# Recurrent mixer of an encoder: score blocks of a forward and a backward direction issued in one run on TensorE, the first run of each pair keeping only its lowest level

## The chip, the cores and the metric

The kernel runs on one NeuronCore of a Trainium2 chip. The metric is the device time of one launch in microseconds (us). The time of the kernel before is the median of three runs, 2628.89 us (2628.30 to 2629.09). About 0.2% of that, 5.3 us, is what a measurement of this kernel can tell from no change.

## The reference, cut to what matters

The kernel computes a two-layer encoder on 1024 tokens of width 1024. Layer 0 is a windowed attention, layer 1 a bidirectional gated linear recurrence; each layer also has four cross-attention heads into 256 memory tokens, and ends with a convolutional gated feed-forward part. Only layer 1's recurrence and its cross-attention heads matter here. The recurrence runs for 8 heads of 128 key and 128 value dimensions, once forward and once backward in time:

```python
def gla_chunked(q, k, v, log_f):
    ...
    b = jnp.cumsum(log_f, axis=2)
    b_end = b[:, :, -1:]
    q_dec = q * jnp.exp(b)
    k_dec = k * jnp.exp(-b)
    k_end = k * jnp.exp(b_end - b)
    causal = np.tril(np.ones((HG_CHUNK, HG_CHUNK), dtype=bool))
    s = jnp.where(causal, jnp.einsum('bcthk,bcshk->bchts', q_dec, k_dec), 0.0)
    o_intra = jnp.einsum('bchts,bcshv->bcthv', s, v)

    def step(state, inp):
        qd, ke, vc, dec = inp
        o = jnp.einsum('bthk,bhkv->bthv', qd, state)
        state = dec[..., None] * state + jnp.einsum('bshk,bshv->bhkv', ke, vc)
        return state, o
...
    o = (gla_chunked(q, k_f, v, lf_f)
         + flip_t(gla_chunked(flip_t(q), flip_t(k_b), flip_t(v), flip_t(lf_b))))
    o = rmsnorm(o, norm_g.reshape(HG_HEADS, HG_VAL_DIM)).reshape(bsz, t, HG_W).astype(u.dtype)
    o = o * jax.nn.silu(gate)
```

All operands are float32.

## The kernel before, in words

The whole program is unrolled in Python and given to a scheduler, which fixes the order of each engine's queue when the program is built: among the instructions whose inputs and buffers are there it takes the one that stands earliest in the program, and `tc.high_priority(AHEAD)` moves instructions ahead by 2000 places. Buffers are named by pool and tag, with a number of copies (`bufs`); the next tile of a tag waits until a copy's last reader is done. Large matrix products are made in three passes of a high and a low part of each operand (`mm3`, lines 84 to 86), because both operands are split into two fp32r tiles.

Layer 1's mixer is `hgrn()` (from line 1023). It goes head by head. `proj(h)` (from line 1137) makes the head's projections in groups of 24 matmuls of 512 columns each: `q` and the two gates `s` (called f and b in `ORD`), each for two halves of 512 tokens, and, for every second head, the values and output gates of two heads. Every group writes a bank of PSUM with the tag `pj`, of which there are two (`psj`, line 1041). A bank is free again when the group's result was read: for `q` by three ScalarE operations and a VectorE multiplication (lines 1091 to 1093 and 1129), for `s` by one VectorE operation (line 1134).

`head(h)` (line 1338) then calls `direction` four times in this order of (direction, half): (0,0), (1,1), (0,1), (1,0); I call these runs 1 to 4. One run computes, for 512 tokens in four chunks `c` of 128, the decay factors on ScalarE and VectorE (lines 1177 to 1228), then the scores of each chunk. The 128x128 score matrix of a chunk is triangular and is built from three levels of blocks: four 32x32 blocks on the diagonal (from `E2` and `E1`; the lowest level), two 32x32 blocks beside them (from `G32`), and one 64x64 block (from `G`) written as two blocks of 32 rows and 64 columns. Each block is one fp32 matmul with 32 rows of output, at one of four column strips of TensorE (`tile_position=(0, i)`, line 1212):

```python
                return pe.matmul(pa[i:i + 32, c, j:j + n], x[:, c * P + i:c * P + i + 32], y[:, c * P + j:c * P + j + n],
                                 start=True, stop=True, tile_position=(0, i))
```

Strip number i/32 is the place of the block's output rows. Lines 1231 to 1246 issue eight blocks a chunk, 32 a run: first, chunk by chunk, the two 64-column blocks, the two diagonal blocks of the other half of the rows and one middle block there; then, again chunk by chunk, the other two diagonal blocks and the other middle block. In one run the 64-column blocks lie in two of the four strips, `far` and `near`: strips 3 and 2 for direction 0, strips 0 and 1 for direction 1. So the strip `far` gets, for each chunk, one block of 64 columns and two of 32, the strip beside it one of 64 and one of 32, and the other two strips two blocks and one block of 32.

After that a masked copy moves the scores from PSUM to `Az` (line 1253, VectorE), and they are stored or added to `As` of the half (line 1257 ScalarE, or 1259 GpSimd). The keys are transposed (line 1262), multiplied with the values (line 1267), and the state `S` is updated on VectorE (line 1276). `output` (line 1279), called for half 1 and then half 0 after all four runs, multiplies `As`, `qin` and `S` (line 1291) into a bank `po`, normalizes, and writes the result.

The decay factors use a ring of five tiles with the tag `E`; a run takes eight of them (`a_`, `L1`, `R`, `B`, `E1`, `E2`, and `G` twice).

Between the runs of every second head stand two units of the cross-attention (`cross`, line 1327; `cross_unit` from line 201): one after run 3, one after run 4. A unit makes its queries in a `pj` bank (24 matmuls), splits them into `xh` and `xl` (lines 214 and 215), multiplies with the memory keys (tile `ps`), takes the softmax, transposes it (line 237), splits it twice into `ph` and `pl` (lines 89 and 90, once for each half of the memory tokens), and multiplies with the memory values (tile `po` or `pu`). `xh`, `xl`, `ph` and `pl` have one buffer each.

The functions that the change touches, with what calls them:

Of the kernel before, what the change touches and what calls it, by code (L numbers as in the profile page):

```python
# [8 lines left out]
F32 = mybir.dt.float32  # L9
F32R = mybir.dt.float32r  # L10
# [3 lines left out]
ALU = mybir.AluOpType  # L14
# [4 lines left out]
P = 128  # L19
# [30 lines left out]
def build(tc, A, out):  # L50
    nc = tc.nc
    act, dve, pool, pe = nc.scalar, nc.vector, nc.gpsimd, nc.tensor
# [970 lines left out]
    def hgrn():  # L1023
# [3 lines left out]
        early = tc.alloc_tile_pool(name="hg0", bufs=1, reuse_waits="tile")  # L1027
# [4 lines left out]
        late = tc.alloc_tile_pool(name="hgv", bufs=1, side="right", reuse_waits="tile")  # L1032
        V, G = [late.tile([P, 3, NT, P], F32, name=x) for x in ("v", "gs")]
        wp = tc.alloc_tile_pool(name="hg1", bufs=1, side="right", reuse_waits="tile")
        for x in ("xh", "xl", "ph", "pl"):
            wp.tile([P, 512], F32R, tag=x, bufs=1, name=x)
        for x in ("kvh", "kvl"):
            wp.tile([P, 2, 256], F32R, tag=x, bufs=1, name=x)
# [22 lines left out]
        gm = [one([P, 512], f"gm{d}", U8) for d in range(2)]  # L1061
# [20 lines left out]
        Az = [one([P, 512], f"Az{d}") for d in range(2)]  # L1082
# [12 lines left out]
        def proj_tm(h, us, ts):  # L1095
# [3 lines left out]
            for t in ts[::2]:  # L1099
# [37 lines left out]
        def proj(h):  # L1137

            r = {"q": [None, None], "s": [[None, None], [None, None]], "v": V[:, h % 3], "gs": G[:, h % 3]}
            us = {}  # L1140
# [18 lines left out]
            r["run"] = run  # L1159
            return r  # L1160

        def direction(h, r, d, b, qin, S, As):

            q, k = r["q"][b], r["s"][d][b]
            rev = slice(None, None, -1) if d else slice(None)
            lt, er = (0, 1) if d else (1, 0)

            def E():
                return early.tile([P, 512], F32, tag="E", bufs=5, name="E")

# [22 lines left out]
            pa = PA[d]  # L1193
            E1, E2 = E(), E()
# [5 lines left out]
            def parts(n):  # L1200
                return halves(EP, n) + halves(ER, n) + halves(q, n) + halves(k, n)
# [8 lines left out]
            def block(c, i, j, x, y, n=32):  # L1210

                return pe.matmul(pa[i:i + 32, c, j:j + n], x[:, c * P + i:c * P + i + 32], y[:, c * P + j:c * P + j + n],
                                 start=True, stop=True, tile_position=(0, i))

            def step(n):
                pl_, pe_, rl_, re_ = parts(n)[:4]
                e = 0 if d else n - 1
                nb = 512 // (2 * n)
                dve.tensor_tensor(re_, re_, bc(pl_[:, :, e:e + 1], [P, nb, n]), op=ALU.mult)
                dve.tensor_tensor(pl_, pl_, bc(pe_[:, :, e:e + 1], [P, nb, n]), op=ALU.mult)  # L1220

            for n in (32, 64):
                step(n // 2)
                G = E()
                gl, ge = halves(G, n)
                pl_, pe_, rl_, re_, ql, qe, kl, ke = parts(n)
                pool.tensor_tensor(gl, pl_, ql, op=ALU.mult)
                dve.tensor_tensor(ge, re_, ke, op=ALU.mult)
                if n == 32:
                    G32 = G  # L1230
            with tc.high_priority(AHEAD):
                far, near, x = er * 64 + er * 32, er * 64 + lt * 32, lt * 64
                mm = None
                for c in range(4):
                    with tc.issue_after(mm.ins) if mm else nullcontext():
                        block(c, far, x, G, G, 64)
                        block(c, near, x, G, G, 64)
                        for o in (0, 32):
                            block(c, x + o, x + o, E2, E1)
                        mm = block(c, x + er * 32, x + lt * 32, G32, G32)  # L1240
                for c in range(4):
                    with tc.issue_after(mm.ins):
                        block(c, far, far, E2, E1)
                        block(c, near, near, E2, E1)
                        mm = block(c, far, near, G32, G32)
            step(64)
            dec = wp.tile([P, 4], F32, tag="dec", bufs=2, name="dec")
            e = 0 if d else P - 1
# [4 lines left out]
            dve.copy_predicated(Az[d], gm[d], pa.rearrange("p c t -> p (c t)"))  # L1253
            a2 = lambda x: x.rearrange("p c t -> p (c t)")
            if As[b] is None:
                As[b] = wp.tile([P, 4, P], F32, tag="As", bufs=2, name="As")
                act.copy(a2(As[b]), Az[d])
            else:
                pool.tensor_tensor(a2(As[b]), a2(As[b]), Az[d], op=ALU.add)
            tp = bank("pt")  # L1260
            for c in range(4):
                pe.transpose(tp[:, c, :], ER[:, c * P:(c + 1) * P], ident)
# [5 lines left out]
            for c in (range(3, -1, -1) if d else range(4)):  # L1268
                cg = 4 * b + c
                nx = cg - 1 if d else cg + 1  # L1270
                if not 0 <= nx < NT:
                    continue
                if cg == (NT - 1 if d else 0):
                    act.copy(S[:, nx, :], pu[:, c, :])
                else:
                    dve.scalar_tensor_tensor(S[:, nx, :], S[:, cg, :], dec[:, c:c + 1], pu[:, c, :],
                                             op0=ALU.mult, op1=ALU.add)

        def output(h, r, b, qin, S, As):
            po = bank("po")  # L1280
# [45 lines left out]

        def cross(n):
            def pair(kind, i):
                return [wp.tile([P, 512], F32R, tag=kind + c, bufs=1, name=kind + c) for c in "hl"]

            for _ in range(n):
                xh_, xb_ = units.pop(0)
                if xhead[1] != xh_:
                    xhead[1] = xh_
                    xhead[0] = cross_head(1, xh_, wp)
                cross_unit(1, xh_, xb_, xhead[0], wp, tags, wp, pair, not units)

# [239 lines left out]
```

## Time and profile before

| What | Value |
|---|---|
| median of 3 runs | 2628.89 us |
| the profiled execution: its own time | 2632.24 us |
| its span, first to last instruction | 2630.4 us |
| granted TensorE clock, mean | 0.998 |
| PE busy over the span | 2593.7 us (99%) |
| DVE busy | 1763.4 us (67%) |
| ACT busy | 1333.4 us (51%) |
| POOL busy | 476.4 us (18%) |
| layer 1's recurrent mixer in the span | from about 1208 to 1890 us |

PE is TensorE's matmul side, PEld its loading of weights, DVE is VectorE, ACT ScalarE, POOL GpSimd. In a row of the time line the first number is the start in us from the span's beginning, the second the duration; then come engine, line, operation, the tiles written and read, and their shapes. A fp32 matmul appears as two records, a weight load and a matmul twice over, so that a run's 32 blocks are 64 matmul records. A row of a query by line gives the count, the shortest, median and longest duration in ns, and the first and last start. The ends of matmuls are modelled, so their starts say more than their durations.

### The profile page before, as it was taken

The numbers are of one execution on the slowest core, as the hardware profiler recorded it, in microseconds if no ns is written. First come the engines' busy times: TensorE is split into PE (matmuls) and PEld (weight loads), VectorE is DVE, ScalarE is ACT, GpSimd is POOL, SyncE is SP. The second block draws the span as 40 slices with busy tenths as digits, with TensorE's granted clock in tenths as the row PEclk, the third lists the DMA queues.
The fourth block names the chain that finished last, engine by engine and source line by source line (L and its number), as shares of the span: only waits on it lengthen the run. The fifth ranks groups of instructions, "written<-read, shape, count | busy, mean of one in ns | idle before, by whom it ended". The sixth has DMA issues, their size and how long they took to land. (4 is left out here: it accounts for less than half of the span.)

```text
span 2630.4 us, 39132 instructions
## 1 busy us (share of the span) xinstructions
PE 2593.7 (99%) x14596; PEld 2174.2 (83%) x14596; DVE 1763.4 (67%) x2807; ACT 1333.4 (51%) x2395; POOL 476.4 (18%) x552
## 2 busy tenths in 40 slices
PE   8999999999999999999999999999999999999998
PEld 7988887888888888887888888888887888888887
DVE  6677775577555664488697796877657665656447
ACT  6566665444444454465555554556434444444453
POOL 0431110211111100032233131222311011110013
PEclk9999999999999999999999999999999999999999
DMA  9782341567787757673246341113337777775666
GB/s 356 258 199 67 103 146 57 168 171 195 192 210 201 198 160 250 194 267 109 70 151 162 75 99 47 55 49 101 120 119 197 190 201 200 205 200 172 215 193 236
DMA packets 203919, 431.18 MB, mean 164 GB/s; under 512 B 20048, under 2 KB 64464, under 8 KB 198096
## 3 DMA queue, kind: packets, MB, share of 16 engines
q1 hardware_dynamic: 169744, 329.30, 38.4%
q0 software_dynamic: 24544, 90.19, 16.4%
q10 hardware_dynamic: 9440, 9.19, 1.1%
q8 instruction: 114, 1.87, 0.3%
q14 instruction: 77, 0.63, 0.1%
HBM read 333.18 MB, written 119.54 MB: 172 GB/s over the span
## 5 line engine op out<-in xcount | busy, mean ns | idle before, releaser
L90 DVE TENSOR_TENSOR wl<-st,wh 128x1024 fp32r<-128x1024 f32 (+1 forms) x238 | 263.3, 1113 | 318.8 <-ACT wh L89 294.4
L89 ACT CAST wh<-st 128x1024 fp32r<-128x1024 f32 (+1 forms) x238 | 222.6, 937 | 293.1 <-PE X L578 194.1
L84 PE MATMUL pj<-uh,wh 128*128 128x512 f32 x512 | 202.9, 397 | 3.6 <-DVE q L1129 2.5
L578 PE MATMUL X<-wl,wh 128*128 128x512 f32 x528 | 204.7, 390 | 0.3 <-DVE wl L90 0.3
L578 PE MATMUL X<-wh,wl 128*128 128x512 f32 x528 | 204.5, 389 | 0.0
L86 PE MATMUL pj<-uh,wl 128*128 128x512 f32 x512 | 202.1, 395 | 0.0
L85 PE MATMUL pj<-ul,wh 128*128 128x512 f32 x512 | 201.0, 393 | 0.1
L578 PE MATMUL X<-wh 128*128 128x512 f32 x528 | 198.7, 390 | 1.4 <-ACT c L992 1.4
L84 PE MATMUL pj<-wh,uh 128*128 128x384 f32 (+1 forms) x512 | 189.0, 370 | 2.5 <-DVE gs L1115 1.9
L86 PE MATMUL pj<-wh,ul 128*128 128x384 f32 (+1 forms) x512 | 187.1, 365 | 0.0
L85 PE MATMUL pj<-wl,uh 128*128 128x384 f32 (+1 forms) x512 | 187.0, 365 | 0.0
L80 DVE TENSOR_TENSOR wl<-st,wh 128x1024 fp32r<-128x1024 f32 (+1 forms) x91 | 119.1, 1316 | 29.7 <-ACT wh L79 28.9
L578 PE MATMUL V<-uh,wh 128*128 128x512 f32 x336 | 130.7, 389 | 0.0
L578 PE MATMUL V<-ul,wh 128*128 128x512 f32 x336 | 130.7, 389 | 0.0
L578 PE MATMUL V<-uh,wl 128*128 128x512 f32 x336 | 130.7, 389 | 0.0
L578 PEld LDWEIGHTS X<-wh 128*128 128x128 f32 x528 | 99.1, 188 | 22.4 <-ACT c L992 1.8
L578 PEld LDWEIGHTS X<-wl,wh 128*128 128x128 f32 x528 | 99.1, 188 | 21.1 <-DVE wl L90 0.7
L578 PEld LDWEIGHTS X<-wh,wl 128*128 128x128 f32 x528 | 99.1, 188 | 20.5
L84 PEld LDWEIGHTS pj<-uh,wh 128*128 128x128 f32 x512 | 96.3, 188 | 23.4 <-DVE q L1129 3.3
L79 ACT CAST wh<-st 128x1024 fp32r<-128x1024 f32 (+1 forms) x97 | 97.5, 1014 | 35.3 <-PE pj L85 22.3
L961 POOL TENSOR_TENSOR c<-c,g 128x512 f32<-128x512 f32 x24 | 42.5, 1789 | 391.2 <-PE X L578 322.1
L85 PEld LDWEIGHTS pj<-ul,wh 128*128 128x128 f32 x512 | 96.3, 188 | 19.3 <-DVE ul L90 0.4
(409 smaller groups left out, 7058.8 us busy)
## 6 DMA issues: line engine op xcount, KB each, us to landing
st<-hid SPq DMA_DIRECT2D x154, 256.0 KB, 3.0
st<-in_ffw_dram SPq DMA_DIRECT2D x108, 256.0 KB, 3.2
w2s<-in_ffw_dram POOLq DMA_DIRECT2D x24, 1024.0 KB, 8.3
st<-in_ffw_dram SPq DMA_DIRECT2D x46, 512.0 KB, 4.2
hid<-tt SPq DMA_DIRECT2D x88, 256.0 KB, 4.8
st<-w2s SPq DMA_DIRECT2D x88, 256.0 KB, 2.8
sx<-in_ffw_dram SPq DMA_DIRECT2D x84, 256.0 KB, 3.9
sy<-in_ffw_dram SPq DMA_DIRECT2D x42, 512.0 KB, 6.6
```

The lines of the kernel that those rows point to most:

```text
L79: act.copy(h[:, :n], raw)
L80: (eng or dve).tensor_tensor(l[:, :n], raw, h[:, :n].bitcast(F32), op=ALU.subtract)
L84: pe.matmul(o, ah, bh, start=first, stop=False)
L85: pe.matmul(o, ah, bl, start=False, stop=False)
L86: return pe.matmul(o, al, bh, start=False, stop=last)
L89: act.copy(h, src)
L90: dve.tensor_tensor(l, src, h.bitcast(F32), op=ALU.subtract)
L578: last = pe.matmul(o, x, y, start=new, stop=e, skip_group_check=not first)
L961: pool.tensor_tensor(y[q][:, t, :], y[q][:, t, :], g3[:, c], op=ALU.mult)
```

## The change

`direction` gets one more argument, `held`, and returns something. Run 1 and run 3 (the first of each pair) are called with `held` None. They issue only the four diagonal blocks of each chunk, 16 blocks, and return three functions: `tops` (the two 64-column blocks of a chunk), `mids` (the two middle blocks) and `masked` (the masked copy and what stores it). Run 2 and run 4, which are of the other direction, get these functions, and issue for each chunk: the first run's two 64-column blocks, their own two, their own four diagonal blocks, the first run's two middle blocks, their own two. That is 12 blocks a chunk, 48 in all, and as the directions differ, the 64-column blocks of the two lie in all four strips, and so do the middle blocks. The masked copies of both runs follow there, the first run's first. The number of blocks of a pair stays 64.

The first run's two `G` tiles must live until the second run's blocks. They get a tag of their own, `H`, with two buffers (4 KB a partition), and no longer come from the ring `E`. To make room, `ph` and `pl` of the cross-attention units lose their own buffers: they now take the tags of `xh` and `xl`, one buffer each.

```diff
-        for x in ("xh", "xl", "ph", "pl"):
+        for x in ("xh", "xl"):
             wp.tile([P, 512], F32R, tag=x, bufs=1, name=x)
...
-        def direction(h, r, d, b, qin, S, As):
+        def direction(h, r, d, b, qin, S, As, held):
...
-                G = E()
+                G = E() if held else early.tile([P, 512], F32, tag="H", bufs=2, name="H")
...
+            def tops(c):
+                for t in (er, lt):
+                    block(c, er * 64 + t * 32, lt * 64, G, G, 64)
+
+            def mids(c):
+                return [block(c, o + er * 32, o + lt * 32, G32, G32) for o in (0, 64)][-1]
+
             with tc.high_priority(AHEAD):
-                far, near, x = er * 64 + er * 32, er * 64 + lt * 32, lt * 64
                 mm = None
                 for c in range(4):
                     with tc.issue_after(mm.ins) if mm else nullcontext():
-                        block(c, far, x, G, G, 64)
-                        block(c, near, x, G, G, 64)
-                        for o in (0, 32):
-                            block(c, x + o, x + o, E2, E1)
-                        mm = block(c, x + er * 32, x + lt * 32, G32, G32)
-                for c in range(4):
-                    with tc.issue_after(mm.ins):
-                        block(c, far, far, E2, E1)
-                        block(c, near, near, E2, E1)
-                        mm = block(c, far, near, G32, G32)
+                        if held:
+                            held[0](c)
+                            tops(c)
+                        for o in range(0, P, 32):
+                            mm = block(c, o, o, E2, E1)
+                        if held:
+                            held[1](c)
+                            mm = mids(c)
...
-            dve.copy_predicated(Az[d], gm[d], pa.rearrange("p c t -> p (c t)"))
-            a2 = lambda x: x.rearrange("p c t -> p (c t)")
...
+            def masked():
+
+                dve.copy_predicated(Az[d], gm[d], pa.rearrange("p c t -> p (c t)"))
+                a2 = lambda x: x.rearrange("p c t -> p (c t)")
...
+            if held:
+                held[2]()
+                masked()
...
+            return None if held else (tops, mids, masked)
...
         def cross(n):
             def pair(kind, i):
-                return [wp.tile([P, 512], F32R, tag=kind + c, bufs=1, name=kind + c) for c in "hl"]
+                return [wp.tile([P, 512], F32R, tag="x" + c, bufs=1, name=kind + c) for c in "hl"]
...
+            held = None
             for i, (d, b) in enumerate(((0, 0), (1, 1), (0, 1), (1, 0))):
-                direction(h, r, d, b, qin[d], S[d], As)
+                held = direction(h, r, d, b, qin[d], S[d], As, held)
```

More of the change, by code (lines that the diff above doesn't have):

```diff
@@ L1252, in direction @@
             dve.tensor_tensor(ER, ER, k, op=ALU.mult)
-            dve.copy_predicated(Az[d], gm[d], pa.rearrange("p c t -> p (c t)"))
-            a2 = lambda x: x.rearrange("p c t -> p (c t)")
[L1255 to L1259, printed above, removed]
+            def masked():
+                dve.copy_predicated(Az[d], gm[d], pa.rearrange("p c t -> p (c t)"))
+                a2 = lambda x: x.rearrange("p c t -> p (c t)")
+                if As[b] is None:
+                    As[b] = wp.tile([P, 4, P], F32, tag="As", bufs=2, name="As")
+                    act.copy(a2(As[b]), Az[d])
+                else:
+                    pool.tensor_tensor(a2(As[b]), a2(As[b]), Az[d], op=ALU.add)
+            if held:
+                held[2]()
+                masked()
             tp = bank("pt")
```

## The prediction, made before the changed kernel was run

> **What bounds the kernel now.** I read the page's head first, then the stage of the recurrent mixer alone, then what TensorE waits for in it, then single runs and units in the time line.
>
> ```profile
> span 2630.4 us, 39132 instructions
> PE 2593.7 (99%) x14596; PEld 2174.2 (83%) x14596; DVE 1763.4 (67%) x2807; ACT 1333.4 (51%) x2395; POOL 476.4 (18%) x552
> ...
> 1208.00:1890.00 682.00, 673.59 (x5303) 568.85 (x5304) 536.31 (x1006) 364.42 (x785) 179.72 (x187) 1.00 0.32 93
> ```
>
> The last line is the mixer's stage in the table of stages: its length, then PE, PEld, DVE, ACT and POOL busy, the granted clock, the DMA share. PE is busy 673.6 of 682 us, DVE 536. So here a microsecond taken out of PE's queue is a microsecond of the kernel, unless PE then waits for something. What it waits for now:
>
> ```profile
> PE pj L84 <- DVE q L1129: 2.5, 2, 2.3
> PE pj L84 <- DVE gs L1115: 1.9, 3, 0.7
> PE pa L1212 <- POOL E L1227: 1.9, 4, 0.7
> PE pj L84 <- DVE s L1134: 1.0, 1, 1.0
> PE pt L1262 <- ACT ot L1321: 0.8, 1, 0.8
> PE pt L121 <- DVE ul L90: 0.3, 1, 0.3
> PE pu L1267 <- DVE S L1276: 0.2, 1, 0.2
> ```
>
> That is 8.6 us in all (total, times, longest). Note the first kind: a projection group that waits until VectorE has read a `pj` bank. One such wait is 2.3 us long. There are two banks, and the change will keep one of them occupied.
>
> **The score blocks.** One run of 32 blocks on PE, and the row of line 1212 over the whole stage:
>
> ```profile
> 1229.67 0.39 PE L86 MATMUL pj<-wh,ul 128*128 128x512 f32 x1
> 1229.90 0.39 PE L84 MATMUL pj<-wh,uh 128*128 128x512 f32 x1
> 1230.21 1.14 PE L1212 MATMUL pa<-E 128*32 128x64 f32 x64
> 1231.28 0.50 PE L84 MATMUL pj<-wh,uh 128*128 128x512 f32 x1
> 1231.62 0.39 PE L85 MATMUL pj<-wl,uh 128*128 128x512 f32 x1
> ...
> 1208.00:1890.00 682.00, 36.43 (x2048) 32.87 (x2048) 1.00 0.32 93
> ```
>
> Projection matmuls start 0.23 us apart (1229.67, 1229.90). Around the run, 1229.90 to 1231.62 is 1.72 us with two steps of 0.23 in it, so a run interrupts the stream for 1.26 us. The 32 runs are 36.43/32 = 1.14 us busy each. Of these, 0.95 us lie between the first and the last start (1.14 less the 0.196 us that the last record takes, next rows). The remaining 0.3 us, getting in and out, stay: the change keeps 32 runs.
>
> What sets the 0.95 us? The whole run, and the part until 1230.69, in the query by line:
>
> ```profile
> L1212 PE MATMUL pa<-E x64: 192/196/243, 1230.2 to 1231.2; 128*32 128x32 f32 x48, 128*32 128x64 f32 x16
> ...
> L1212 PE MATMUL pa<-E x39: 193/217/243, 1230.2 to 1230.7; 128*32 128x32 f32 x23, 128*32 128x64 f32 x16
> ```
>
> By 1230.69, after 0.48 us, 39 of the 64 records have begun, among them all 16 wide ones. The other 25, all narrow, take the other 0.47 us. So the run does not go at a rate per matmul. It goes by its fullest strip: `far` has 16 narrow records after its 8 wide ones (two per block). If the second part is that strip's 16 narrow records, a narrow one holds a strip for about 0.03 us; the first part is its 8 wide ones, 0.056 us each: 8 x 0.056 + 16 x 0.031 = 0.95. The other strips run beside it and are done early.
>
> After the change run 1 has 8 narrow records in each strip: 8 x 0.031 = 0.25 us. Run 2 has in each strip 8 wide and 16 narrow: 0.95 us, as a run has now, but with no strip idle. A pair goes from 1.90 to 1.20 us, and 16 pairs (8 heads, two each) give **11.2 us less on PE**. The other end of this price: at the average rate of today, 0.95/64 = 15 ns a record, the unchanged 128 records of a pair would cost 1.90 us and the gain is nothing; at the rate of the first part (0.48/39 = 12.3 ns) 1.57 us and 5.2 us in all. I take 11.2, since the two parts of the run are explained by the strip and not by the count. A rule of the Trainium skill speaks for the other end: "TensorE: Matmul & The Clock Gate", "Wait — 56ns, not 53.3ns?", says that starts of matmuls never come closer than about 25 ns however few columns they have; then a pair's 128 records would cost 3.2 us before and after, and the sum would be that of the last rival below. The trace's 15 ns on average contradicts it for matmuls in different strips.
>
> **The cross-attention's buffers.** `ph` and `pl` now live in `xh` and `xl`. Within one unit that costs nothing: the transposed softmax needs all scores, and these are the last readers of `xh`. But units come in twos. The second unit's queries are made right behind the first's, and today are split at once. Head 0, with the stage's count of units:
>
> ```profile
> L214 ACT ACTIVATE xh<-pj x8: 589/597/618, 1283.9 to 1782.4; 128x512 fp32r<-128x512 f32 x8
> ...
> 1291.52 0.39 PE L86 MATMUL pj<-uh,wl 128*128 128x512 f32 x1
> 1292.67 0.59 ACT L214 ACTIVATE xh<-pj 128x512 fp32r<-128x512 f32 x1
> 1293.95 0.68 DVE L215 SCALAR_TENSOR_TENSOR xl<-pj,xh 128x512 fp32r<-128x512 f32 x1
> ...
> 1294.75 1.22 DVE L232 TENSOR_TENSOR xp<-xp,rd 128x1024 f32<-128x1024 f32 x1
> ...
> 1296.98 0.39 PE L86 MATMUL pj<-uh,wl 128*128 128x512 f32 x1
> 1297.21 0.39 PE L84 MATMUL pj<-uh,wh 128*128 128x512 f32 x1
> 1297.41 0.60 ACT L1091 ACTIVATE q<-pj 128x512 f32<-128x512 f32 x1 [3.24 <-PE pj L86]
> 1299.37 0.69 DVE L1129 TENSOR_TENSOR q<-pj,q 128x512 f32<-128x512 f32 x1 [3.40 <-ACT q L1093]
> 1300.61 1.03 PE L237 MATMUL pt<-ident,xp 128*128 128x128 f32 x8
> 1303.76 0.69 DVE L1134 TENSOR_SCALAR s<-pj 128x512 f32<-128x512 f32 x1 [1.20 <-PE pj L86]
> 1313.33 0.39 PE L86 MATMUL po<-ph,kvl 128*128 128x512 f32 x1
> ```
>
> The second unit's last query matmul starts at 1291.52; its split ends at 1294.63, which frees its bank. The first unit's last reader of `ph` and `pl` starts at 1313.33. With shared tags the second split must wait for that reader, and its bank stays full for up to 20 us. The next head's groups, which alternate between two banks, have one. The group for `q` ends at about 1297.2 (1296.98 and a step); today the group for `s` starts at 1297.21 in the other bank. Then it has to wait for the multiplication that ends at 1300.06: **2.85 us**. The transposes of line 237 (0.8 us to issue) may go there and leave 2.0. After `s` the next group waits for the operation at 1303.76, 0.7 to 0.8 us, partly covered by key transposes and by the first unit's own matmuls; the wait after that is either none (the second unit's bank is free by then) or up to another 2.85. What is queued behind PE's wait is everything, since PE's queue is in order; ScalarE and VectorE have the split itself to wait for, but the scheduler puts it where it is ready.
>
> There are 8 units, so 4 such events. One costs from 0.5 us (transposes, output and key matmuls fill nearly everything) to 2.85 + 0.8 + 2.85 = 6.5 us; I take 2.7 (2.0 and most of 0.8), nearest to the 2.3 us in the list of waits, which is one wait of the same kind. **Four events: 10.8 us more**, from 2 to 26.
>
> **The small parts.** The ring `E` gives a first run six tiles instead of eight, and the narrow blocks release theirs early:
>
> ```profile
> ACT E L1178 <- PE pa L1212: 11.9, 7, 3.3
> ...
> L1253 DVE COPY_PREDICATED Az<-gm,pa x32: 722/734/748, 1231.4 to 1866.7; 128x512 f32<-128x512 uint8 x32
> L1257 ACT COPY As<-Az x16: 603/620/622, 1232.3 to 1839.1; 128x512 f32<-128x512 f32 x16
> L1259 POOL TENSOR_TENSOR As<-As,Az x16: 1276/1640/2172, 1261.3 to 1867.5; 128x512 f32<-128x512 f32 x16
> ...
> 1364.35 0.39 PE L1291 MATMUL po<-v,As 128*128 128x128 f32 x2
> 1371.73 1.14 PE L1212 MATMUL pa<-E 128*32 128x64 f32 x64
> ```
>
> ScalarE waited 7 times, 11.9 us, for the blocks before it could start the next run's factors. Second runs of a pair will start theirs earlier, and the 1.9 us in which PE waited at its blocks for POOL's part of `E` can go. I take 1.5 us off, from 0 to 2.
>
> The masked copy of a first run moves behind the second run's last factors, past one run's work in the queues of DVE (0.73 us), ACT (0.62) or POOL (1.64). Behind it on VectorE stand the transposes' and the state's operations, 0.73 us later in runs 2 and 4 and as much earlier in runs 1 and 3. `output` of half 1, of which head 1 issued some matmuls (1364.35) ahead of run 4's blocks (1371.73), now has to wait for these and two masked copies and an addition more. I cost this at nothing: projection groups of the next head, or in head 7 of the output projection, stand ready for PE; without that cover it would be 0.73 + 1.64 = 2.4 us a head. GpSimd's DMA issues go behind `qin`, which is not moved.
>
> **The sum**: -11.2 + 10.8 - 1.5 = -1.9 us on the profiled 2632.24 us (span 2630.4 and 1.8 around it), so 2630.3; the median is 3.35 below the profiled execution, so **2627.0 us** in the median's terms.
>
> **The rivals.**
> - *The gain shows.* The scheduler, with an idle PE, brings the first unit's transposes and both `po` products forward, and the second bank is free after one group. Then an event costs 1 us or less, and the sum is -11.2 + 4 x 1 - 1.5 = -8.7: 2620 us. For it: the softmax was ready at 1295.97 (1294.75 and 1.22) and its transposes came only at 1300.61, so there is work to bring forward. Against it: nothing but 0.8 us of it is ready when the bank is missing.
> - *The held bank decides.* If an event costs more than (11.2 + 1.5 + 5.3)/4 = 4.5 us, the kernel is slower by over 5.3 us. This needs two waits for a `q` bank in an event, 2.85 + 2.85 or near it. At 6.5 us the sum is +13.3, at 5.5 it is +9.3: 2638 us. For it: the groups come in the order q, s, q, and the first unit's products are placed late today (1313.33).
> - *The change does not do what it says:* the blocks cost by their number. This is what the Trainium skill's 25 ns would mean too. Then the gain is nothing, and the sum is +10.8 - 1.5 = +9.3: 2638 us. For it only that four strips with a wide block each are not seen today; against it the two parts of the run.
>
> **How the numbers follow.** 0.2% of the kernel is 5.3 us, about what its measurement can tell from no change. The forecast, within 5.3 us either way, 0.47. The gain shows: 0.29. The held bank decides: 0.19. Cost by number: 0.05. Faster 0.29, same 0.47, slower 0.24. The likeliest case's own range is 2623.6 to 2634.2. The whole range goes from 2617.5 (events at 0.5 us, -11.2 + 2 - 2) to 2638.5 (either slow rival at 9.3 to 9.6); it leaves out events of 6 us and more.
>
> **What would show it.** In the profile after: line 1212's busy time falls from 36.4 us by about 11; a first run has 32 records within 0.25 us of starts, a second run 96 within about 0.95. Were the second run's 96 to take 1.4 us, the strip theory is wrong. PE's list of waits shows `pj` waiting for `q` (line 1129) or `s` four times or more, each 2 to 3 us, behind each second unit, and its idle time in the stage rises from 8.4 to about 17 us. If these waits are missing, the time is near 2620. The split of the second unit should come just behind the first unit's last `po` matmul. If PE's idle time grows in other places, above all in heads 1, 3, 5 and 7, the part that I costed at nothing was wrong.

## The result and the profile after

The changed kernel takes 2658.86 us (median of 4 runs, 2657.43 to 2660.78) against 2628.99 us for the kernel before (4 runs, 2628.30 to 2629.26). The ratio is 1.0114, with an interval from 1.0097 to 1.0132: it is slower by about 30 us. I had forecast 2627.0 us and a range up to 2638.5, so the prediction was wrong. The profiled execution took 2660.78 us.

From line 1231 on the changed file's line numbers are shifted. The transposes of `ER` are line 1272 (before 1262), `pu` is 1277 (1267), the state update 1286 (1276), `ER` times k is 1256 (1252), the masked copy 1259 (1253), `on` 1309 (1298). `ER` then holds a run's decayed keys, which PE transposes; `gs` are the output gates, whose line 1115 reads a `pj` bank; `on` is the normalized output, which PE transposes too. The factors (1177 to 1228) and the blocks (1212) kept theirs.

The head of the page after, then the mixer's stage, which is 30 us longer, in the table of stages (length, busy time of PE, PEld, DVE, ACT and POOL, granted clock, DMA share), and line 1212 alone over the same stretch:

```profile
span 2659.0 us, 39186 instructions
PE 2601.3 (98%) x14596; PEld 2172.6 (82%) x14596; DVE 1758.6 (66%) x2807; ACT 1331.0 (50%) x2395; POOL 481.5 (18%) x552
```

```profile
1208.00:1920.00 712.00, 681.89 (x5297) 566.84 (x5297) 531.47 (x1004) 361.19 (x784) 182.85 (x186) 0.98 0.30 89
...
1208.00:1920.00 712.00, 30.57 (x2048) 25.68 (x2048) 0.98 0.30 89
```

PE sat idle for 712.00 - 681.89 = 30.1 us of the stage, where it was 8.4 before. The granted clock, 1.00 before, is 0.98: something has throttled it. The blocks' busy time did fall, from 36.43 to 30.57 us. PE's waits in the stage after (total, times, longest):

```profile
PE pt L1313 <- DVE on L1309: 10.8, 2, 5.7
PE pt L1272 <- DVE ER L1256: 6.8, 3, 2.3
PE pj L84 <- DVE gs L1115: 6.0, 1, 6.0
PE pj L84 <- DVE s L1134: 2.3, 5, 1.0
PE po L84 <- ACT ph L89: 1.2, 4, 0.3
PE pb L84 <- ACT v L490: 1.1, 1, 1.1
PE po L85 <- DVE pl L90: 0.9, 4, 0.2
```

Six long waits carry it: three of some 2.3 us for `ER` and three of 5 to 6 us for `gs` or `on`. None of these kinds was long before. The first of them, in head 1's third run, in the time line of the kernel after (start, duration, engine, line, operation):

```profile
1355.01 0.62 ACT L1178 ACTIVATE E<-E 128x512 f32<-128x512 f32 x1
...
1357.10 0.68 DVE L1180 SCALAR_TENSOR_TENSOR s<-s,E 128x512 f32<-128x512 f32 x1
...
1357.70 0.46 PE L1212 MATMUL pa<-E 128*32 128x32 f32 x32
1357.70 0.68 DVE L1182 TENSOR_TENSOR E<-E 128x512 f32<-128x512 f32 x1
...
1358.64 0.41 DVE L1228 TENSOR_TENSOR H<-ER,s 128x256 f32<-128x256 f32 x1
...
1358.98 1.75 DVE L1184 TENSOR_TENSOR_SCAN E<-smask,E 128x512 f32<-128x512 bf16 x1
...
1360.58 0.36 PE L1212 MATMUL pa<-H 128*32 128x64 f32 x8
...
1360.89 0.41 DVE L1219 TENSOR_TENSOR ER<-ER,EP 128x256 f32<-128x256 f32 x1
...
1361.23 0.68 DVE L1187 TENSOR_TENSOR E<-E 128x512 f32<-128x512 f32 x1
...
1362.42 0.68 DVE L1256 TENSOR_TENSOR ER<-ER,s 128x512 f32<-128x512 f32 x1
...
1363.25 0.63 PE L1272 MATMUL pt<-ident,ER 128*128 128x128 f32 x4 [2.31 <-DVE ER L1256]
```

Line 1272 waits for the third run's `ER`, made at 1362.42. In front of that, on VectorE, stand four operations of the fourth run's factors (1180, 1182, 1184, 1187: 0.68 + 0.68 + 1.75 + 0.68 = 3.8 us). They could stand there because ScalarE had made the fourth run's logarithm (1178) at 1355.01, ahead of the third run's blocks at 1357.70. The same place in the time line of before has the other order:

```profile
1354.54 0.68 DVE L1252 TENSOR_TENSOR ER<-ER,s 128x512 f32<-128x512 f32 x1
...
1356.83 1.14 PE L1212 MATMUL pa<-E 128*32 128x64 f32 x64
...
1358.23 0.61 ACT L1178 ACTIVATE E<-E 128x512 f32<-128x512 f32 x1
```

There `ER` comes first, then the blocks, and only then the next run's logarithm, which needed a tile of the ring `E` that the blocks release.

To add up, I compared in each trace the steps from one matmul's start to the next in the heads' stage (first projection of head 0 to the end of the output projection) with the median step between the same operand widths in before (the blocks of line 1212, of either width, count as one kind). A surplus over 0.05 us counts as wait, or, up to 0.5 us and under a granted clock below 1, as half clock; the rest is almost all blocks. Two traces by this reckoning, in us:

| | stage | waits | half clock | rest (blocks) | normal steps |
|---|---|---|---|---|---|
| before | 792.5 | 24.3 | 0 | 16.0 | 752.2 |
| after | 823.7 | 51.0 | 11.1 | 7.7 | 753.9 |

The blocks gave 8.3 us. Waits took 26.7 and the half clock 11.1 (and 1.7 went to a changed mix of steps): 31.2 us. Outside the stage the profiled execution was some 3 us shorter, which leaves the 28.6 us between the spans.

### The profile page after: what moved, and what is told of

Its sections match the earlier page's. It is cut to its first block, busy times and chain, and to the rows that moved or that the text cites. A ratio compares the mean times of both kernels' runs of the same rounds, so it can differ in the third digit from the quotient of the medians.

```text
span 2659.0 us, 39186 instructions
## 1 busy us (share of the span) xinstructions
PE 2601.3 (98%) x14596; PEld 2172.6 (82%) x14596; DVE 1758.6 (66%) x2807; ACT 1331.0 (50%) x2395; POOL 481.5 (18%) x552
## 5 line engine op out<-in xcount | busy, mean ns | idle before, releaser
L80 DVE TENSOR_TENSOR wl<-st,wh 128x1024 fp32r<-128x1024 f32 (+1 forms) x91 | 116.4, 1286 | 22.4 <-ACT wh L79 21.5
L86 PEld LDWEIGHTS pj<-uh,wl 128*128 128x128 f32 x512 | 97.0, 190 | 19.5 <-issue 0.4
```

The lines of the kernel that those rows point to most:

```text
L80: (eng or dve).tensor_tensor(l[:, :n], raw, h[:, :n].bitcast(F32), op=ALU.subtract)
L86: return pe.matmul(o, al, bh, start=False, stop=last)
```

## The experiments

My theory after the result, "early factors": the tight ring `E` had been a throttle. When the first run's `G` moves to tag `H`, the second run's factors can start earlier, and the scheduler puts them in the in-order queues of VectorE and ScalarE ahead of operations that PE waits for. Its rivals were, in turn, the shared buffers (my prediction's main cost), the late masked copies with `output` behind them, the scattered blocks, and the mere deferral of blocks to the second run. The expectations of the first runs call the theory by its first form, "ring". A VectorE that has become slower as a whole is not among the rivals: it is busy 1758.6 us in the execution after, 1763.4 before.

The last column of the table is read from the order of VectorE's instructions: in how many of the 32 runs the first VectorE factor of the next run (1180) stands ahead of this run's `ER`. Waits, half clock and rest are as in the table above, each from one execution, 4.4 us longer than the median for the changed kernel with its factors held, at most 3.3 us off it for the others. Each ratio is to runs of before that were taken along with the kernel (medians 2628.06 to 2629.45 us).

| kernel | median us | ratio (interval) | waits | half clock | rest | `ER` behind next run |
|---|---|---|---|---|---|---|
| before | 2628.99 | | 24.3 | 0 | 16.0 | 0 |
| after | 2658.86 | 1.0114 (1.0097 to 1.0132) | 51.0 | 11.1 | 7.7 | 11 |
| shared buffers alone | 2629.27 | 1.0002 (0.9992 to 1.0011) | 25.4 | 0 | 15.6 | 0 |
| masks late alone | 2629.35 | 1.0002 (0.9992 to 1.0011) | 24.3 | 0 | 15.8 | 0 |
| shared and `H`, old blocks | 2634.53 | 1.0019 (1.001 to 1.0029) | 29.8 | 0 | 15.9 | 8 |
| after, one burst a run | 2661.96 | 1.0124 (1.0107 to 1.0141) | 57.3 | 12.4 | 4.4 | 11 |
| first pair only | 2636.37 | 1.003 (1.0019 to 1.0041) | 36.5 | 1.6 | 9.9 | 3 |
| second pair only | 2637.17 | 1.0029 (1.0017 to 1.0041) | 37.9 | 0 | 9.8 | 8 |
| first pair, seven tiles, no `H` | 2648.11 | 1.0066 (1.0049 to 1.0083) | 44.3 | 5.1 | 10.1 | 5 |
| shared, seven tiles, old blocks | 2649.24 | 1.0076 (1.0059 to 1.0092) | 41.7 | 3.8 | 15.5 | 0 |
| after, factors held by `ER` | 2632.09 | 1.001 (1.0001 to 1.002) | 33.4 | 1.6 | 7.6 | 0 |
| one burst, factors held by `ER` | 2626.12 | 0.9989 (0.998 to 0.9998) | 32.7 | 1.6 | 4.4 | 0 |
| one burst, released early | 2658.87 | 1.0121 (1.0104 to 1.0138) | 55.0 | 9.2 | 4.5 | 7 |
| shared and `H`, factors held by `ER` | 2628.73 | 1.0003 (0.9994 to 1.0013) | 24.4 | 0 | 15.4 | 0 |

### The two other parts, each alone

Shared buffers alone, on the kernel before:

```diff
-        for x in ("xh", "xl", "ph", "pl"):
+        for x in ("xh", "xl"):
...
-                return [wp.tile([P, 512], F32R, tag=kind + c, bufs=1, name=kind + c) for c in "hl"]
+                return [wp.tile([P, 512], F32R, tag="x" + c, bufs=1, name=kind + c) for c in "hl"]
```

> The kernel before, with one part of the change alone: ph and pl live in the tags of xh and xl; nothing else is moved. Theory 'held bank' (a second cross-attention unit keeps its pj bank until the first unit's last reader): four events of 1 to 3 us, so 2633 to 2641 us, with PE's waits on pj, po and pt grown there. Theory 'ring' (the new waits come from the tag H, which takes two tiles out of the ring E): about 2629 to 2633 us, and none of the waits of 2 us and more that the changed kernel shows in heads 1 to 6. Theory 'scattered blocks': the same as the ring theory here.

It cost nothing: ratio 1.0002. The time line of this kernel at head 0's second unit shows why:

```profile
1298.17 0.49 PE L84 MATMUL po<-ph,kvh 128*128 128x512 f32 x1 [0.29 <-ACT ph L89]
...
1305.45 0.39 PE L86 MATMUL po<-ph,kvl 128*128 128x512 f32 x1
1305.88 0.60 ACT L214 ACTIVATE xh<-pj 128x512 fp32r<-128x512 f32 x1 [5.14 <-PE po L86]
```

The unit's products with `ph` start from 1298.17 to 1305.45; in before the last of them started at 1313.33. The scheduler had brought them forward. So the second split starts at 1305.88, 13 us later than in before (1292.67) and not 21, and PE waits 0.29 us for `ph`. In the whole stage its waits for `ph` and `pl` come to 2.1 us, and the 2.5 us of waits for `q` of before are gone. The held bank decides nothing here.

Masks late alone, on the kernel before (the first run's masked copy and its copy into `As` wait for the second run, in both pairs):

```diff
+            def masked():
...
+            if held:
+                held()
+                masked()
...
+            return None if held else masked
```

> The kernel before with one thing moved: the masked copy of the first run of each pair, with what stores it, comes behind the second run's blocks, as in the changed kernel. Blocks, rings and cross-attention buffers are those of before. Theory 'late output': this alone makes most of the loss, 2648 us or more, with output of half 1 behind run 4's blocks. Theory 'deferred blocks' or a loss from the blocks' new order: within 6 us of the kernel before.

Also nothing: 1.0002, with the waits of before to the tenth. A later masked copy and `output` are not the cause by themselves.

### One burst a run

In the changed kernel PE's stream is interrupted by 44 bursts of blocks, not 32: in 12 second runs the first run's two wide blocks of chunk 0 start alone (the 8 records at 1360.58 above), as nothing holds them back. This version puts the second run's own two wide blocks of chunk 0 first and ties all else behind them:

```diff
-                mm = None
+                mm = tops(0) if held else None
...
-                            tops(c)
+                            if c:
+                                tops(c)
```

> The changed kernel, with the second run's own two 64-column blocks of the first chunk put first and all other blocks queued behind them, so that no held block can be issued alone: 32 bursts of blocks instead of 44. Theory 'scattered blocks': the 12 extra bursts cost 0.5 us each and bring PE to the waits behind them early; without both the time falls to 2630 us or less. Theory 'ring': only the 12 x 0.5 = 6 us go, so about 2653 us, and the waits of 5 to 6 us stay.

The blocks got 3.3 us cheaper (rest 7.7 to 4.4) and the time did not: 2661.96 us, as waits rose from 51.0 to 57.3. Neither time forecast held, neither 2630 us or less nor my own theory's 2653; its waits of 5 to 6 us did stay. The extra bursts are a real but small cost and not the cause.

### `H` alone, and each pair alone

The first edit keeps the blocks of before on top of the shared buffers; the other two pack the blocks of one pair of a head only, in one burst.

```diff
-                G = E()
+                G = early.tile([P, 512], F32, tag="H", bufs=2, name="H") if first else E()
...
-                direction(h, r, d, b, qin[d], S[d], As)
+                direction(h, r, d, b, qin[d], S[d], As, i in (0, 2))
```

> The kernel before with the shared tags and with the G tiles of the first run of each pair in the tag H; the score blocks are issued as before, 32 a run, and nothing is deferred. Theory 'ring': the second run's factors start early here too, so most of the loss is here: 2650 us or more, with waits of 5 us behind VectorE in heads 2, 4 and 6 and a lowered clock after them. Theory 'scattered blocks' or 'deferral' (the loss comes from where the blocks and the masked copies are put): within 5 us of the run with shared tags alone.

```diff
-                held = direction(h, r, d, b, qin[d], S[d], As, held)
+                held = direction(h, r, d, b, qin[d], S[d], As, held, i not in (0, 1))
```

> The changed kernel with the blocks of runs 1 and 2 of each head taken together (in one burst), and runs 3 and 4 as in the kernel before, each with its own blocks and its own masked copy. Theory 'late output' (the scores of half 1 are complete only after run 4, so output of half 1 starts behind run 4, the one po bank hands over to half 0 some 10 us later, and the next head's qin and S wait for that): with runs 3 and 4 as before the long waits go, and half of the packing's gain, 8 x 0.70 = 5.6 us, stays: 2624 to 2631 us. Theory 'deferred blocks' (any first run that keeps its blocks for later upsets the queues): half of the loss stays, about 2645 us.

```diff
-                held = direction(h, r, d, b, qin[d], S[d], As, held)
+                held = direction(h, r, d, b, qin[d], S[d], As, held, i not in (2, 3))
```

> The reverse: runs 1 and 2 as in the kernel before, the blocks of runs 3 and 4 taken together in one burst. Theory 'late output': all of the loss is here, 2655 to 2668 us, with the waits of 2 and of 5 to 6 us at the same places. Theory 'deferred blocks': about 2645 us.

Extra memory without any change of the blocks is 5 us slower. My theory had 2650 us or more here; 2634.53 lies much nearer to what its rival, the place of the blocks, had (within 5 us of the shared buffers' 2629.27). `ER` is overtaken in 8 runs, yet PE's list has no wait for it: its waits, 4.4 us more than with the shared buffers alone, are of other kinds, 2.7 us of them four waits for `q`. So the extra memory alone makes only a small part of the loss.

Each pair alone saves about 6 us on blocks (16.0 to 9.9 and 9.8), but adds 12.2 and 13.6 us of waits, for +7 and +8 us in all. None of the four times forecast (2624 to 2631, 2655 to 2668, about 2645 twice) held. The kernel to set beside them is the one-burst version, since each of them takes its pair's blocks in one burst: there both pairs together add 33.0 us of waits, against 25.8 apart. The half clock adds up even less: 1.6 and 0 apart, 12.4 together. Two loosened pairs in a row thus cost more than the two singly; why is open.

### The ring alone

If a loose ring is the cause, a looser one without `H` must cost as well. First on the version that packs the first pair only:

```diff
-                return early.tile([P, 512], F32, tag="E", bufs=5, name="E")
+                return early.tile([P, 512], F32, tag="E", bufs=7, name="E")
...
-                G = E() if held or alone else early.tile([P, 512], F32, tag="H", bufs=2, name="H")
+                G = E()
```

> As the kernel with the first pair alone taken together, but without the tag H: the ring E has seven tiles, the same memory, and the G tiles come from it. The tag H alone cost about 5 us with the blocks as before. If that came from H's two tiles being tied up, seven free tiles give it back: 2620 to 2626 us. If it came from the second run's factors starting early, seven tiles let them start earlier still, and nothing is won: 2629 us or more.

It is 12 us slower than with five tiles and `H`, as the second of the two expectations has it. Then the ring alone, on the version with shared buffers, with the blocks and masks of before:

```diff
-                return early.tile([P, 512], F32, tag="E", bufs=5, name="E")
+                return early.tile([P, 512], F32, tag="E", bufs=7, name="E")
```

> Before with shared ph/pl and xh/xl and a ring E of seven tiles in place of five; blocks, masked copies and G as before. On VectorE's queue every run's ER still stands in front of the next run's factors. Theory 'early factors' as order in the queues: as the order stays, the time stays, 2627 to 2633 us, ratio 0.9995 to 1.0015. Rival 'loose ring' (whatever starts earlier because tiles are free sooner costs time, in any order): 2636 or more, as the first pair alone rose by 12 us with seven tiles.

Here my expectation was wrong. The kernel is 20 us slower, though every `ER` stands ahead of the next run's factors. The rival's number held: a looser ring costs time by itself. The time line shows another operation overtaken:

```profile
1354.39 1.78 DVE L1180 SCALAR_TENSOR_TENSOR s<-s,E 128x512 f32<-128x512 f32 x1
...
1356.09 0.68 DVE L1129 TENSOR_TENSOR q<-pj,q 128x512 f32<-128x512 f32 x1
...
1356.69 0.71 DVE L1276 SCALAR_TENSOR_TENSOR S<-S,dec,pu 128x128 f32<-128x128 f32 x2
1357.33 0.69 DVE L1182 TENSOR_TENSOR E<-E 128x512 f32<-128x512 f32 x1
1357.93 0.34 DVE L1276 SCALAR_TENSOR_TENSOR S<-S,dec,pu 128x128 f32<-128x128 f32 x1
...
1358.42 1.13 PE L1267 MATMUL pu<-v,kT 128*128 128x128 f32 x8 [2.23 <-DVE S L1276]
```

The state updates of an earlier run, which free the bank `pu`, stand behind the next run's 1180 (1.78 us long here) and 1182, and PE waits 2.23 us. In the version with shared buffers alone all three updates come ahead of this run's `ER` in VectorE's order. There are three such waits, 7.2 of the 16.3 us by which waits rose. Five for `gs` come to 5.7 us, where the version with shared buffers alone has 0.9; in front of the `gs` for which PE waits until 1408.45, five factors of the next run (1180 to 1206) stand on VectorE. So the overtaken `ER` is a mark of the trouble and not all of it: an overtaken `S`, or an overtaken operation that frees a `pj` bank, will do.

### Holding the factors back

The decisive test leaves blocks, `H`, masks and shared buffers as in the changed kernel and only gives the second run's logarithm an operand from the first run's `ER`: a column that is 0 times `ER` plus 1, in place of the constant 1.

```diff
-            act.activation(L1, a_, AF.Ln, bias=1.0)
+            act.activation(L1, a_, AF.Ln, bias=held[3] if held else 1.0)
...
-            dec = wp.tile([P, 4], F32, tag="dec", bufs=2, name="dec")
+            dec = wp.tile([P, 8], F32, tag="dec", bufs=2, name="dec")
...
+            if not held:
+                dve.tensor_scalar(dec[:, 4:5], ER[:, :1], 0.0, 1.0, op0=ALU.mult, op1=ALU.add)
...
-            return None if held else (tops, mids, masked)
+            return None if held else (tops, mids, masked, dec[:, 4:5])
```

> The changed kernel with one data dependency more: the second run of a pair takes the constant 1 in its logarithm (L1178) from a column that VectorE derives from the first run's finished ER, so that its factors can't be queued in front of the first run's last steps. On VectorE's queue the changed kernel has the factors of eight second runs and more in front of the ER of the run before; here no run has. Theory 'early factors' (the second run's factors, started early because the first run hands no tile of the ring E to its G, delay ER, the evacuations and output): PE's waits in the heads' stage fall from 51.0 us to 24 to 30, the half clock of 11.1 us goes, the strips' gain of 8.3 us stays, some 2 us for 12 extra bursts are in it already: 2618 to 2626 us, ratio 0.996 to 0.999 to before. Rival 'deferred blocks' (it is that a second run carries 64 blocks and two masked copies in one piece): the waits stay above 45 us and the time above 2650.

27 of the 30 us are gone (2632.09). Waits fall to 33.4 us, the half clock to 1.6. PE's list has no wait left for `ER` or `on`, and of those for `s` and `gs` this:

```profile
PE pj L84 <- DVE s L1134: 3.6, 5, 1.1
PE pj L84 <- DVE gs L1115: 0.8, 3, 0.3
```

The forecast of 24 to 30 us of waits, and with it of 2618 to 2626 us, was too hopeful, so the gain of the blocks does not show yet. The rival "deferred blocks" falls: the second run still carries the 16 deferred blocks, 48 in all (not the 64 of my expectation), and both masked copies.

The same lines on the version with one burst a run:

> The same dependency as in the run on the changed kernel, in the version whose second run issues its own wide blocks of chunk 0 first and all else behind them, so that there are 32 bursts, not 44. Theory 'early factors': the strips' gain is 11.6 us in place of 8.3, so 2615 to 2624 us, 2 to 4 us below the run on the changed kernel. Rival 'deferred blocks': above 2650.

2626.12 us, 35.8 us less than the same version without the dependency (2661.96). It is some 3 us faster than the kernel before, with an interval that just excludes no change, and still within the 0.2% that I had set as what can be told. It is the best version found, but slower than the 2615 to 2624 us that I expected. Its stage is 790.0 us against 792.5: the blocks save 11.6 (16.0 to 4.4) and normal steps 0.8, waits take back 8.4 and the half clock 1.6. The same rows for it as above for after:

```profile
1208.00:1888.00 680.00, 668.17 (x5305) 559.73 (x5306) 524.72 (x1020) 364.99 (x786) 180.69 (x188) 1.00 0.32 94
...
1208.00:1888.00 680.00, 26.11 (x2048) 22.55 (x2048) 1.00 0.32 94
```

```profile
PE pj L84 <- DVE s L1134: 5.3, 4, 1.5
PE pb L84 <- ACT oh L89: 2.8, 1, 2.8
```

Line 1212 is down to 26.11 us, and of the waits for `ER`, `gs` and `on` nothing long is left. What remains is one wait of 2.8 us in the output projection and four for `s`. In the time line one of these stands behind a factor that now waits for ScalarE:

```profile
1357.41 0.68 DVE L1256 TENSOR_TENSOR ER<-ER,s 128x512 f32<-128x512 f32 x1
...
1358.27 0.14 DVE L1258 TENSOR_SCALAR dec<-ER 128x1 f32<-128x1 f32 x1
...
1359.27 0.69 DVE L1180 SCALAR_TENSOR_TENSOR s<-s,E 128x512 f32<-128x512 f32 x1 [0.53 <-ACT E L1178]
1359.88 0.68 DVE L1134 TENSOR_SCALAR s<-pj 128x512 f32<-128x512 f32 x1
```

Is it the order, or would any added dependency do? The next version takes the column from `EP` in place of `ER`:

```diff
+            if not held:
+                dve.tensor_scalar(dec[:, 4:5], EP[:, :1], 0.0, 1.0, op0=ALU.mult, op1=ALU.add)
             pool.tensor_copy(dec[:, :4].unsqueeze(2), EP.rearrange("p (c t) -> p c t", t=P)[:, :, e:e + 1])
...
             dve.tensor_tensor(ER, ER, k, op=ALU.mult)
-            if not held:
-                dve.tensor_scalar(dec[:, 4:5], ER[:, :1], 0.0, 1.0, op0=ALU.mult, op1=ALU.add)
```

> The one-burst version with the same kind of dependency, but the constant 1 for the second run's logarithm is taken from the first run's EP after its last factor step, one VectorE instruction ahead of ER. On VectorE's queue the second run's factors of the second pair then stand in front of the first run's ER again, as in the changed kernel. Theory 'early factors' as an order in the queues: PE waits 45 to 57 us in the heads' stage, half clock back, 2645 to 2662 us, ratio 1.006 to 1.0125. Rival 'any dependency that delays the second run is enough, or the number of chains in flight decides': within 3 us of the version released by ER, 2623 to 2630 us.

It went as the order theory says: 2658.87 us. One detail of my expectation was not so. Column 0 of `EP` is not touched by the factor steps of these runs, so it is final long before the last step, and the scheduler released the second run much earlier than "one instruction ahead". In head 1's third run the column comes first, then the next run's factor, and `ER` last, 10 places behind that factor; in the rows of the version held by `ER`, above, the factor comes last:

```profile
1350.96 0.15 DVE L1254 TENSOR_SCALAR dec<-EP 128x1 f32<-128x1 f32 x1
...
1355.19 0.68 DVE L1180 SCALAR_TENSOR_TENSOR s<-s,E 128x512 f32<-128x512 f32 x1
...
1360.51 0.68 DVE L1258 TENSOR_TENSOR ER<-ER,s 128x512 f32<-128x512 f32 x1
```

So this run shows that an added dependency is not enough by itself. It doesn't part the order from the early start, since both came back together. PE's waits are back, of the same kinds as after:

```profile
PE pj L84 <- DVE gs L1115: 12.8, 4, 6.2
PE pt L1274 <- DVE ER L1258: 5.6, 3, 2.6
PE pt L1315 <- DVE on L1311: 4.3, 1, 4.3
```

Last, the dependency on the version with shared buffers, `H` and the old blocks:

```diff
-            act.activation(L1, a_, AF.Ln, bias=1.0)
+            act.activation(L1, a_, AF.Ln, bias=held if held is not None else 1.0)
...
+            if first:
+                dve.tensor_scalar(dec[:, 4:5], ER[:, :1], 0.0, 1.0, op0=ALU.mult, op1=ALU.add)
```

> Shared ph/pl and xh/xl and the first runs' G in tag H, blocks as before, with the second run's logarithm released by the first run's ER. Theory 'early factors': the 5 us that the tag H cost (2634.5 against 2629.3) go, as the order on VectorE's queue is again that of before; waits 24 to 27 us, 2627 to 2631 us. Rival 'H costs by its own place, or the dependency costs time itself': 2633 or more.

2628.73 us, the 5 us of `H` are gone and the waits (24.4) are those of before. So neither the tag nor the dependency costs anything by itself. What costs is that the next run's factors start early, and the order in the queues that this makes.

## Why the prediction was wrong

**The step that failed** is the smallest term of the sum: "Second runs of a pair will start theirs earlier [...] I take 1.5 us off, from 0 to 2." I saw that ScalarE's seven waits, 11.9 us, held the factors back, and read an engine's wait as a loss that could only shrink. ScalarE was 51% busy and not on PE's path; its wait was what kept VectorE's queue in the right order. The range for this term had no positive end. In its place stand 26.7 us more of waits and 11.1 us of half clock. Holding the factors back removes 17.6 and 9.5 of them, and 26.8 us of the median; in the one-burst version it removes 35.8 us. So the term is some 27 us or more, with the other sign. What the held version still waits for over before stays open (below). The runs with a changed ring and the old blocks (+5 and +20 us) show the same kind of loss with nothing else changed but the shared buffers, which cost nothing.

The in-order queue, on which this rests, shows in the time line above. The last step of `ER` before its product with k (line 1219 at 1360.89) needs nothing from VectorE that starts later than the operation at 1358.64, and yet it comes behind the scan at 1358.98, which belongs to a run that nobody waits for yet. The Trainium skill ("TensorE: Matmul & The Clock Gate", "Architectural detail: the array is 16× 32×32, not 1× 128×128") calls the queues of ScalarE and VectorE strict FIFO, and no row here speaks against it.

**The held bank** (+10.8 us, from 2 to 26) was wrong in size too: about nothing, by the run with shared buffers alone. The rival "the gain shows" had its reason right (the scheduler brings the products forward) and the forecast's list of `q` waits never appeared.

**The strips** were right. (By the code the wide blocks of direction 0 lie in strips 0 and 1 and those of direction 1 in 3 and 2, the other way round than the description above says; the four strips fill all the same.) A first run's 32 records start within 0.26 us (0.46 in the row at 1357.70, less 0.2 for the last one). A second run has 88, as 8 of its 96 had started earlier. Here in the query by line for the kernel after, they start within 0.94 us by the trace:

```profile
L1212 PE MATMUL pa<-E x64: 192/196/243, 1399.2 to 1400.2; 128*32 128x32 f32 x48, 128*32 128x64 f32 x16
...
L1212 PE MATMUL pa<-H x24: 196/216/243, 1399.4 to 1400.2; 128*32 128x64 f32 x12, 128*32 128x32 f32 x12
```

I had 0.25, and 0.95 for all 96; where these go in one burst, in the one-burst version, they start within 0.98 us. Narrow blocks in four strips thus start every 8 ns (0.26/32). The Trainium skill's floor of about 25 ns (same page, "Wait — 56ns, not 53.3ns?") does not hold across strips, and the rival "cost by number" falls. But "the change keeps 32 runs" was wrong: 12 more bursts cost the 3.3 us that the one-burst version got back. Line 1212 fell by 5.9 us, not 11; without the extra bursts it fell by 10.3.

**Costed at nothing:** the masked copies were indeed worth nothing alone. My last sentence named idle time in heads 1, 3, 5 and 7 as a sign. It came in heads 1, 3 and 5 (the waits for `ER`), and in heads 2, 4 and 6 as well; the cause was not the one that I had put there.

**Open:** how the single waits of 5 to 6 us in heads 2, 4 and 6 divide. Before the one for `gs` (until 1410.91) VectorE does seven factors of the next run, 1180 to 1209. Two of them are also slow there, 1180 with 1.65 and 1182 with 2.54 us, where the median of 1182 is 0.69. How much of the wait is the order and how much the slowness, no run tells. Open are also the 8 to 9 us of waits that the held versions still have over before: the largest are named above, the rest is scattered. And no run parts the order in the queues from the early start that makes it.

## What to carry to other kernels

A wait for a buffer on an engine that is off the critical path can be what keeps in-order queues in a good order; price its loss like any other term, with both signs. Before you loosen a ring, list what the released work will stand in front of in each queue, and price the operation behind it that the bottleneck engine needs. If a change frees work too early, a cheap true dependency (one column, 0.14 us) can restore the order: here it took back 27 of 30 us, though not all waits.

## What the runs showed of the hardware

After some short idles of PE, its granted clock was halved for some microseconds. In the time line after, behind the wait that ended at 1363.25, matmuls of the same form first start 0.23 us apart (1364.43, 1364.66), then 0.43:

```profile
1364.43 0.40 PE L85 MATMUL pj<-ul,wh 128*128 128x512 f32 x1
...
1364.96 0.63 PE L84 MATMUL pj<-uh,wh 128*128 128x512 f32 x1
...
1365.39 0.63 PE L85 MATMUL pj<-ul,wh 128*128 128x512 f32 x1
...
1365.82 0.63 PE L86 MATMUL pj<-uh,wl 128*128 128x512 f32 x1
```

Two stretches of the stages view after show the granted clock (the last three columns: clock, DMA share, rate):

```profile
1364.90:1368.10 3.20, 3.20 (x9) 2.46 (x8) 3.06 (x9) 2.23 (x4) 1.69 (x3) 0.50 0.71 241
...
1411.00:1416.00 5.00, 5.00 (x12) 3.95 (x13) 4.43 (x9) 2.29 (x5) 0.00 (x0) 0.50 1.00 197
```

The trace has five such stretches in the stage after, 3.41 us long behind two of the three waits of 2.3 us and 6.83 around the ends of those of 5 to 6 us, 27.3 us in all. The Trainium skill (same page, "What's actually happening") names a free-running window of 3413 ns, and the lengths agree. It also says that the throttle comes after a whole idle window; here half clock followed 2.31 us of idle at 1363.25, but no half clock followed 2.31 us at 1517.93 in before, and what decides between the two stays open.

Some VectorE operations stretch: line 1182 takes 0.69 us as a rule (median) and up to 2.54 in the kernel after, at 1403.31, beside a multiplication (line 1255) and DMA issues of GpSimd. That the one slows the other was not tried.
